# Block 2's S5 recurrence: scan instructions between two rotations, with a table of rotations made on GpSimd

## The chip, the core and the metric

The kernel runs on one core of one Trainium2 chip. Time is microseconds (us) of device time for one execution; less is better. The core has five engines, each with its own queue of instructions in a fixed order: TensorE (PE in the profile; its weight loads PEld), VectorE (DVE), ScalarE (ACT), GpSimd (POOL) and SyncE (SP), which issues most DMA transfers. An engine takes its next instruction when all earlier ones of its queue have begun and the semaphores that it waits for are up.

## What is computed

Two transformer blocks over 256 tokens and 2048 channels, in fp32. Block 1: differential attention and RWKV-7, gated branches, a gated FFN. Block 2: a mixer of S5, stick-breaking attention and NSA, cross attention, a convolutional FFN. The change touches S5, and by the order of instructions the gated branches of block 1. Cut to these:

```python
# block 1
mix = (gates[..., :D_MODEL] * (o_a @ w_branch_a[l])
       + gates[..., D_MODEL:] * (o_b @ w_branch_b[l])) @ w_out[l]
# block 2: S5, a diagonal complex state per group: 32 groups x 64 states, 256 steps
delta = jnp.exp(log_dt)[:, None]
mag = jnp.exp(lr * delta)
ar = mag * jnp.cos(li * delta)
ai = mag * jnp.sin(li * delta)
xr_in = jnp.einsum('btgc,gpc->btgp', ug, br)
xi_in = jnp.einsum('btgc,gpc->btgp', ug, bi)
_, _, sr, si = lax.associative_scan(_complex_affine, (a_r, a_i, xr_in, xi_in), axis=1)
y = jnp.einsum('btgp,gcp->btgc', sr, c_re) - jnp.einsum('btgp,gcp->btgc', si, c_im)
```

The states obey x(t) = a x(t-1) + b(t) with the same complex a at all steps. The 2048 complex states are 16 tiles of 128.

## The kernel before

**Products.** Every large fp32 product is three products in a format that TensorE runs faster: a weight tile W (128 x 1024 numbers, 512 KB) is read by SP, ScalarE copies it to WH (L163), VectorE makes the rest WL = W - WH (L164), and TensorE multiplies WH with both parts of the activations and WL with the high part (L146 to L148 in `gemm_steps`, L210, L211, L213 in `gemm_t`). So TensorE needs a split of VectorE for each W tile.

**Order.** The program is written as generators. Each `yield` of a gemm is a tick, and a tick advances six lanes of side work that were put there by `spawn`. From what is written so, a scheduler makes one static order for each engine, by its own estimate of when an instruction can run and by priorities (splits and evictions have a high one). An instruction can so come out ahead of the code that surrounds it in the program. `drain` ticks on until a lane is empty.

**Block 1, `mix1` (L973).** `w_br_b`'s outputs are gated and kept in `tb`. Then `w_br_a` runs in 8 blocks nb of 256 columns. Behind each block come two times: ScalarE copies a half of the result (L990), VectorE adds the other (L991), GpSimd multiplies with the gate tile `gr` (L992, tile `md`, four buffers), VectorE adds `tb` (L1025), ScalarE and VectorE make the high and the low part for the next gemm, `w_out` (L1026, L1027). The lane 3 runs `params()` meanwhile: block 2's S5 parameters (L1457 is their helper) and NSA's biases, kept in a DRAM tensor `pd`. The FFN, `ffn1` (L1132), follows.

**Block 2, S5 (`s5`, L1553).** `states()` makes the inputs b of the 16 tiles (TensorE, L1572), copied to SBUF by ScalarE (L1575). `scan(0)` runs the recurrence of nine tiles on VectorE, `scan(1)` that of seven on GpSimd, both with the helper `cma` (L1593), eight operations for one complex multiply-add: 15 steps inside 16 chunks of 16 tokens (128x144 and 128x112 elements), 15 steps from chunk to chunk (128x9 and 128x7), and a correction of all tokens (128x450 and 128x225), 280 operations on VectorE and 272 on GpSimd. `out()` multiplies with C. The lanes run this beside block 2's first gemm and beside stick-breaking attention (L1948 and following) and the compression of NSA's keys (L1891 to L1906; L1900 on VectorE makes the input of L1906).

Of the kernel before, what the change touches and what calls it, by code (L numbers as in the profile page):

```python
# [33 lines left out]
S5_V = 9  # L34
S5_Y = ((2, 1, 4), (2, 1, 6))
# [7 lines left out]
class K:  # L43
# [1088 lines left out]
    def ffn1(self, fp, xr, xa):  # L1132
        nc, tc = self.nc, self.tc
        acc = fp.tile([128, 2, D], F32, tag="acc", name="acc2")
        fin = self.post_norm(fp, acc, "g_ffn_post")
        parts = [range(0, 4), range(4, 8), range(8, 11)]
        first = True
        for pi, blocks in enumerate(parts):
# [43 lines left out]
            def ev_o(nb, P, hs=(0, 1)):  # L1182
                if pi == 2:
                    return fin(nb, P, hs, add=True)
                for h in range(2):
# [3 lines left out]
                    else:  # L1189
# [259 lines left out]
    def s5_params(self, sp):  # L1449
# [39 lines left out]
        PW = S([128, 2, 16, 16], "s5pw")  # L1489
        PR, PI = PW[:, 0], PW[:, 1]  # L1490
        ar, ai = PR[:, :, 0], PI[:, :, 0]
        tt(ar, mg, cs, mul)
        tt(ai, mg, sn, mul)
        tmp = [S([128, 16, 16], f"s5t{k}") for k in range(2)]

        def cmul(o, a, b, n):
            x, y = tmp[0][:, :, :n], tmp[1][:, :, :n]
            tt(x, a[0], b[0], mul)
            tt(y, a[1], b[1], mul)
            tt(o[0], x, y, sub)  # L1500
            tt(x, a[0], b[1], mul)
            tt(y, a[1], b[0], mul)
            tt(o[1], x, y, add)
        n = 1
        while n < 16:
            last = tuple(p[:, :, n - 1:n].to_broadcast([128, 16, n]) for p in (PR, PI))
            cmul((PR[:, :, n:2 * n], PI[:, :, n:2 * n]), (PR[:, :, 0:n], PI[:, :, 0:n]), last, n)
            n *= 2
            yield 3
# [30 lines left out]
        BT = S([128, 4, 2, 128], "s5bt")  # L1540
# [9 lines left out]
        for name, t in (("pw", PW), ("c2", C2), ("bt", BT)):  # L1550
            self.pd_out(name, t)

    def s5(self, sp):  # L1553
# [12 lines left out]
        def states():
            for t in [n for m in range(8) for n in (S5_V + m if S5_V + m < 16 else None, m) if n is not None] + list(range(8, S5_V)):
                p = int(t >= S5_V)
                q, kt = t % 4, t // 4
                ps = self.pst()  # L1570
                for k in range(2):
                    nc.tensor.matmul(ps[:, k * 256:k * 256 + 256], BT[32 * q:32 * q + 32, kt, k], uT[32 * q:32 * q + 32, kt],  # L1572
                                     start=True, stop=True, tile_position=(32 * q, 0))
                for k in range(2):
                    nc.scalar.activation(X[p][k][:, t - parts[p][1]], ps[:, k * 256:k * 256 + 256], AF.Copy)  # L1575
                yield

        def scan(p):
            E, n0, n1 = parts[p]
            n = n1 - n0  # L1580
            ts = slice(n0, n1)
            mul, add, sub = ALU.mult, ALU.add, ALU.subtract
            tmp = [S([128, 450], f"s5t{p}{k}") for k in range(2)]
            x5 = [x.rearrange("p t (c i) -> p t c i", c=16) for x in X[p]]

            def cma(dst, src, cf, shape):

                a = [tm[:, :math.prod(shape)] for tm in tmp]
                v = [q.rearrange("p (a b c) -> p a b c", a=shape[0], b=shape[1]) if len(shape) > 2 else
                     q.rearrange("p (a b) -> p a b", a=shape[0]) for q in a]  # L1590
                for o, a, b, op in ((v[0], src[0], cf[0], mul), (v[1], src[1], cf[1], mul), (dst[0], dst[0], v[0], add), (dst[0], dst[0], v[1], sub),
                                    (v[0], src[1], cf[0], mul), (v[1], src[0], cf[1], mul), (dst[1], dst[1], v[0], add), (dst[1], dst[1], v[1], add)):
                    E.tensor_tensor(o, a, b, op=op)  # L1593
            ab = [q[:, ts, 0:1].to_broadcast([128, n, 16]) for q in (PR, PI)]
            for i in range(1, 16):
                cma([x[:, :, :, i] for x in x5], [x[:, :, :, i - 1] for x in x5], ab, [n, 16])
                yield S5_Y[p][0]
            a16 = [q[:, ts, 15:16] for q in (PR, PI)]
            for c in range(1, 16):
                cma([x[:, :, c, 15:16] for x in x5], [x[:, :, c - 1, 15:16] for x in x5], a16, [n, 1])  # L1600
                yield S5_Y[p][1]
            for t0 in range(0, n, 2):
                m = min(2, n - t0)
                tl, tg = slice(t0, t0 + m), slice(n0 + t0, n0 + t0 + m)
                cma([x[:, tl, 1:16, 0:15] for x in x5],
                    [x[:, tl, 0:15, 15:16].to_broadcast([128, m, 15, 15]) for x in x5],
                    [q[:, tg, None, 0:15].to_broadcast([128, m, 15, 15]) for q in (PR, PI)], [m, 15, 15])
                yield S5_Y[p][2]
# [2 lines left out]
        def scans():
            self.spawn(3, scan(0))
            self.spawn(4, scan(1))
            yield
# [713 lines left out]
```

## Time and profile before

| | us |
|---|---|
| median of 3 runs (lowest, highest) | 3426.7 (3416.67, 3427.69) |
| the profiled execution | 3433.04 |
| its span in the trace | 3431.3 |
| TensorE busy | 3297.2 |
| VectorE busy | 2269.6 |
| GpSimd busy | 686.9 |

The span runs from the first to the last instruction of the trace; the execution's own time is 1.7 us longer. [...] In a timeline each row is one instruction, or several of one kind in a row (x2), with its start, its length, and in brackets how long the engine stood idle before it and what it waited for.

### The profile page before, as it was taken

To read this page: it belongs to the slowest core of one execution; us is meant where nothing else is said; L and a number is where in the kernel's file an instruction comes from. 1 tells how busy PE (TensorE), PEld (TensorE's weight loads), DVE (VectorE), ACT (ScalarE), POOL (GpSimd) and SP (SyncE) were. 2 spreads that over 40 slices of the span, in tenths; PEclk is the share of its full clock that TensorE was granted. 3 is DMA by queue.
4 is the path that set the end of the run, shared out by engine and by line. 5 is a ranking of instruction groups with operands and counts; after the bars stand their busy time and mean duration, and the time that the engine had idled before them with its cause. 6 is when DMAs were issued, how large, how long until landed. Compare 5 with 4: busy or idle time off the path is not lost.

```text
span 3431.3 us, 50392 instructions
## 1 busy us (share of the span) xinstructions
PE 3297.2 (96%) x18954; PEld 2743.5 (80%) x18954; DVE 2269.6 (66%) x3636; ACT 1710.4 (50%) x2675; POOL 686.9 (20%) x882
## 2 busy tenths in 40 slices
PE   8999999999999999999999999789999999999998
PEld 7887877877888888888888877567677888888886
DVE  5776787756667656545555565986777675666576
ACT  5545455444545445444444444256545554454453
POOL 0203123421111201100100113920121321111021
PEclk9999999999999999999999999989999999999999
DMA  6553544646556774566566564336356466666664
GB/s 215 155 176 102 160 133 130 194 155 215 185 176 226 236 257 135 184 191 190 186 190 192 187 223 144 99 106 207 125 184 207 135 185 191 188 187 192 190 186 154
DMA packets 177765, 607.04 MB, mean 177 GB/s; under 512 B 22427, under 2 KB 27372, under 8 KB 176752
## 3 DMA queue, kind: packets, MB, share of 16 engines
q1 hardware_dynamic: 168800, 580.25, 53.8%
q0 software_dynamic: 7856, 21.94, 2.0%
q8 instruction: 149, 2.44, 0.3%
q10 hardware_dynamic: 864, 1.62, 0.1%
q14 instruction: 96, 0.79, 0.1%
HBM read 584.29 MB, written 22.59 MB: 177 GB/s over the span
## 4 chain that ended last, share of the span: by engine, by line
PE 72%; DVE 8%; issue 8%; DMA 3%; ACT 2%; POOL 1%; DVEq 0%; POOLq 0%; ACTq 0%; SPq 0%
PE pm L211 25%; PE pm L210 12%; PE pm L146 9%; PE pm L147 9%; PE pm L148 9%; DVE WL L164 2%; PE ps L65 1%; DVE s5x L1593 1%; ACT WH L163 1%; PE pm L213 1%; DMA T<-dT 1%; DVE s5t L1593 1%; PE ps L1572 0%; DMA dT<-TM 0%; PE ps L1854 0%
## 5 line engine op out<-in xcount | busy, mean ns | idle before, releaser
L164 DVE TENSOR_TENSOR WL<-W,WH 128x1024 fp32r<-128x1024 f32 (+2 forms) x1016 | 1268.1, 1249 | 863.6 <-ACT WH L163 858.1
L211 PE MATMUL pm<-HL,WH 128*128 128x512 f32 x4928 | 1745.5, 401 | 8.8 <-ACT WH L163 4.0
L163 ACT ACTIVATE WH<-W 128x1024 fp32r<-128x1024 f32 (+2 forms) x1016 | 1066.9, 1051 | 1059.4 <-PE pm L148 444.7
L210 PE MATMUL pm<-HL,WL 128*128 128x256 f32 x4620 | 1313.6, 284 | 8.4 <-DVE WL L164 6.4
L211 PEld LDWEIGHTS pm<-HL,WH 128*128 128x128 f32 x4928 | 913.2, 189 | 212.6 <-DVE pt L496 7.7
L210 PEld LDWEIGHTS pm<-HL,WL 128*128 128x128 f32 x4620 | 875.3, 189 | 35.7 <-DVE WL L164 10.4
L147 PE MATMUL pm<-WL,HL 128*128 128x512 f32 (+1 forms) x1472 | 579.4, 394 | 17.5 <-DVE WL L164 17.5
L146 PE MATMUL pm<-WH,HL 128*128 128x512 f32 (+1 forms) x1472 | 585.4, 399 | 1.2 <-ACT WH L163 1.2
L148 PE MATMUL pm<-WH,HL 128*128 128x512 f32 (+1 forms) x1472 | 577.0, 392 | 0.7 <-DVE HL L1097 0.7
L147 PEld LDWEIGHTS pm<-WL,HL 128*128 128x128 f32 x1472 | 278.4, 189 | 79.1 <-DVE WL L164 23.3
L146 PEld LDWEIGHTS pm<-WH,HL 128*128 128x128 f32 x1472 | 277.7, 189 | 60.0 <-ACT WH L163 2.0
L148 PEld LDWEIGHTS pm<-WH,HL 128*128 128x128 f32 x1472 | 278.2, 189 | 58.3 <-DVE HL L1097 1.1
L2122 POOL TENSOR_TENSOR fcv<-fcv,fcv 128x256 f32<-128x256 f32 x44 | 51.8, 1176 | 547.4 <-DVE fcv L2109 547.4
L1155 POOL TENSOR_TENSOR sg<-sg,spr 128x256 f32<-128x256 f32 x44 | 45.9, 1060 | 391.2 <-ACT sg L1154 391.2
L213 PE MATMUL pm<-HL,WL 128*128 128x256 f32 x308 | 87.0, 282 | 0.8 <-DVE WL L164 0.8
L1164 POOL TENSOR_TENSOR HL<-fu,HL 128x256 fp32r<-128x256 f32 x44 | 48.3, 1118 | 195.2 <-ACT HL L1163 195.2
L1593 POOL TENSOR_TENSOR s5t<-s5x,PW 128x112 f32<-128x112 f32 (+3 forms) x136 | 71.8, 547 | 60.8 <-ACT s5x L1575 60.8
L2108 DVE SCALAR_TENSOR_TENSOR fcv<-fu,cw,fcv 128x255 f32<-128x255 f32 x88 | 53.1, 603 | 32.6 <-ACT fcv L2107 32.6
L2107 ACT ACTIVATE fcv<-fu,cw 128x256 f32<-128x256 f32 x88 | 52.4, 596 | 40.2 <-DVE fu L2106 40.2
L213 PEld LDWEIGHTS pm<-HL,WL 128*128 128x128 f32 x308 | 58.5, 190 | 13.5 <-DVE WL L164 1.5
L1593 POOL TENSOR_TENSOR s5x<-s5x,s5t 128x112 f32<-128x112 f32 (+3 forms) x136 | 68.7, 527 | 0.2
L1593 DVE TENSOR_TENSOR s5x<-s5x,s5t 128x144 f32<-128x144 f32 (+3 forms) x140 | 66.2, 473 | 1.5
(504 smaller groups left out, 3218.3 us busy)
## 6 DMA issues: line engine op xcount, KB each, us to landing
W<-in_w_ffi SPq DMA_DIRECT2D x176, 512.0 KB, 3.6
W<-in_w_up SPq DMA_DIRECT2D x176, 512.0 KB, 4.1
W<-in_w_rkv SPq DMA_DIRECT2D x96, 512.0 KB, 3.5
W<-in_w_qkv SPq DMA_DIRECT2D x96, 512.0 KB, 3.6
W<-in_w_ffo SPq DMA_DIRECT2D x88, 512.0 KB, 3.5
W<-in_w_down SPq DMA_DIRECT2D x88, 512.0 KB, 4.3
W<-in_w_gate SPq DMA_DIRECT2D x64, 512.0 KB, 4.1
W<-in_w_out SPq DMA_DIRECT2D x64, 512.0 KB, 4.3
```

The costliest lines, as they stand in the source:

```text
L146: nc.tensor.matmul(o, a, WH[:, j], start=(k == 0), stop=False)
L147: nc.tensor.matmul(o, a, WL[:, j], start=False, stop=False)
L148: nc.tensor.matmul(o, b, WH[:, j], start=False, stop=(k == kts - 1))
L163: self.nc.scalar.activation(WH, W, AF.Copy)
L164: self.gated(self.nc.vector.tensor_tensor(WL, W, WH.bitcast(F32), op=ALU.subtract))
L210: nc.tensor.matmul(o[:, 0, ts], WL[:, kk, c], x[:, 0, ts], start=False, stop=False)
L211: nc.tensor.matmul(o[:, :, ts], WH[:, kk, c], x[:, :, ts], start=(k == 0), stop=(k == 15))
L213: nc.tensor.matmul(o[:, 0, ts], WL[:, kk, c], x[:, 0, ts], start=False, stop=False)
L1593: E.tensor_tensor(o, a, b, op=op)
L2107: nc.scalar.activation(c, u, AF.Identity, scale=cw[:, 2, ct:ct + 1], bias=cw[:, 3, ct:ct + 1])
L2108: nc.vector.scalar_tensor_tensor(c[:, 1:], u[:, 0:255], cw[:, 1, ct:ct + 1], c[:, 1:], op0=ALU.mult, op1=ALU.add)
L2122: nc.gpsimd.tensor_tensor(c, c, gs[i], op=ALU.mult)
```

## The change

- The parameters: besides the magnitude `mg` of a, VectorE makes `un`, the unit rotation of a and its powers 2, 4, ..., 128, each brought back to length one. Both go to `pd`. The powers 1 to 16 of a, `pw`, go.
- `s5_table` (new, spawned on lane 3 at the start of `ffn1`): GpSimd makes the unit rotations of all 256 steps for the 16 tiles, in 8 groups of two tiles, by doubling: from n steps to 2n with four operations, two of 4n elements and two of 2n, for n = 1 to 128. Each group ends with a DMA of 512 KB into `pd` from GpSimd's queue. Each `yield 3` is three ticks.
- `s5`: for each tile, VectorE turns the inputs back by the table (two products of 128x512 with the result in PSUM, two of 128x256), runs two real scans along the 256 tokens (`tensor_tensor_scan`, with `mg` as factor), and GpSimd turns them forward again (two products of 128x512, two of 128x256). GpSimd also issues the 16 loads of 256 KB of the table. The copies by ScalarE and the recurrence by `cma` go. The work of a pair of tiles is spread over ticks by `S5_Y`, four ticks a tile.

```diff
-S5_V = 9
-S5_Y = ((2, 1, 4), (2, 1, 6))
+S5_Y = (1, 1, 2)
...
     def ffn1(self, fp, xr, xa):
         nc, tc = self.nc, self.tc
         acc = fp.tile([128, 2, D], F32, tag="acc", name="acc2")
+        self.spawn(3, self.s5_table())
...
+        self.drain(3)
         z = self.hl_both(self.hA)
...
+        self.pd_out("mg", mg)
+
+        un = S([128, 8, 2, 16], "s5un")
+        V.tensor_copy(un[:, 0], u)
+        for n in range(1, 8):
+            a, b, c, d = un[:, n - 1, 0], un[:, n - 1, 1], un[:, n, 0], un[:, n, 1]
+            tt(t0, a, a, mul)
+            tt(t1, b, b, mul)
+            tt(c, t0, t1, sub)
+            V.scalar_tensor_tensor(d, a, 2.0, b, op0=mul, op1=mul)
+            tt(t0, c, c, mul)
+            tt(t1, d, d, mul)
+            tt(t0, t0, t1, add)
+            V.tensor_scalar(t0, t0, -0.5, 1.5, op0=mul, op1=add)
+            tt(c, c, t0, mul)
+            tt(d, d, t0, mul)
+            yield 3
+        self.pd_out("un", un.rearrange("p n k t -> p (n k t)"))
...
+    def s5_table(self):
+
+        nc = self.nc
+        mul, add, sub = ALU.mult, ALU.add, ALU.subtract
+        ro = PD_OFF["rot"][0]
+        with self.tc.tile_pool(name="rt", bufs=1, reuse_waits="tile", side="right") as sp:
+            un = sp.tile([128, 8, 2, 16], F32, name="s5un")
+            self.pd_in(un.rearrange("p n k t -> p (n k t)"), "un")
+            yield 3
+            for g in range(8):
+                gs = slice(2 * g, 2 * g + 2)
+                R = sp.tile([128, 2, 2, 256], F32, tag="R", bufs=2, name=self.nm("s5rt"))
+                nc.gpsimd.memset(R[:, :, 0, 0:1], 1.0)
+                nc.gpsimd.memset(R[:, :, 1, 0:1], 0.0)
+                for k in range(8):
+                    n = 1 << k
+                    a, b = (sp.tile([128, 2, 2, 128], F32, tag=t, name=self.nm("s5ro"))[:, :, :, :n] for t in "ab")
+                    cb, sb = (un[:, k, x, gs, None, None].to_broadcast([128, 2, 2, n]) for x in range(2))
+                    R0, R1 = R[:, :, :, 0:n], R[:, :, :, n:2 * n]
+                    for o, x, y, op in ((a, R0, cb, mul), (b, R0, sb, mul), (R1[:, :, 0], a[:, :, 0], b[:, :, 1], sub),
+                                        (R1[:, :, 1], a[:, :, 1], b[:, :, 0], add)):
+                        nc.gpsimd.tensor_tensor(o, x, y, op=op)
+                    yield 3
+                nc.gpsimd.dma_start(self.pd[:, ro + 1024 * g:ro + 1024 * g + 1024], R.rearrange("p t k n -> p (t k n)"))
...
+        def rot(t):
+            R = sp.tile([128, 2, T], F32, tag="s5r", bufs=4, name=self.nm("s5r"))
+            nc.gpsimd.dma_start(R, self.pd[:, ro + 512 * t:ro + 512 * t + 512].rearrange("p (k t) -> p k t", k=2))
+            return R
...
+                    nc.vector.tensor_tensor(a, p3, cb, op=mul)
+                    nc.vector.tensor_tensor(b, p3, sb, op=mul)
+                    yield S5_Y[0]
+                    nc.vector.tensor_tensor(a[:, 0], a[:, 0], b[:, 1], op=add)
+                    nc.vector.tensor_tensor(a[:, 1], a[:, 1], b[:, 0], op=sub)
+                    yield S5_Y[1]
+                    for k in range(2):
+                        nc.vector.tensor_tensor_scan(a[:, k], mg[:, t:t + 1].to_broadcast([128, T]), a[:, k], 0.0, op0=mul, op1=add)
+                    nc.gpsimd.tensor_tensor(X[:, t], a, cb, op=mul)
+                    nc.gpsimd.tensor_tensor(b, a, sb, op=mul)
+                    nc.gpsimd.tensor_tensor(X[:, t, 0], X[:, t, 0], b[:, 1], op=sub)
+                    nc.gpsimd.tensor_tensor(X[:, t, 1], X[:, t, 1], b[:, 0], op=add)
+                    yield S5_Y[2]
```

The lines of `mix1` stand one lower in the changed kernel: L992 is L991 there, L1025 is L1024, L164 is L163.

**What moves.** GpSimd's queue in `w_br_a`, before, from the gate products (`md`) of block nb = 4 to those of nb = 7 and what follows them:

```order
L992 TENSOR_TENSOR md_11405<-md_11405,gr_11313 128x256
L992 TENSOR_TENSOR md_11412<-md_11412,gr_11313 128x256
L992 TENSOR_TENSOR md_11511<-md_11511,gr_11419 128x256
...
L992 TENSOR_TENSOR md_11723<-md_11723,gr_11631 128x256
L992 TENSOR_TENSOR md_11730<-md_11730,gr_11631 128x256
L1081 TENSOR_TENSOR xr<-xr,acc_11749 128x512 x2
```

The same queue now, from the end of the table's fourth group (`s5rt` is the table, `s5ro` its products) and nb = 4 to the first product of nb = 5:

```order
L1586 TENSOR_TENSOR s5ro_14137<-s5rt_13813,s5un 128x512
L991 TENSOR_TENSOR md_11460<-md_11460,gr_11368 128x256
L1586 TENSOR_TENSOR s5rt_13813<-s5ro_14136,s5ro_14137 128x2x128 x2
L1588 DMA pd<-s5rt_13813 128x1024
L991 TENSOR_TENSOR md_11467<-md_11467,gr_11368 128x256
L1586 TENSOR_TENSOR s5ro_14176<-s5rt_14173,s5un 128x4
...
L1586 TENSOR_TENSOR s5ro_14798<-s5rt_14535,s5un 128x512
L991 TENSOR_TENSOR md_11566<-md_11566,gr_11474 128x256
```

Between the second product of nb = 4 and the first of nb = 5 now stand the table's fifth and most of its sixth group. The first table operation comes behind the first product of nb = 2, the last DMA ahead of the two products of nb = 7; no table operation is left behind them, in the FFN.

VectorE's queue in the same stage, before, at block nb = 5 (L991 and L1025 lie before and behind GpSimd's product, WL is a split):

```order
L991 TENSOR_TENSOR md_11511<-pm_11421,md_11511 128x256
L1025 TENSOR_TENSOR md_11511<-md_11511,tb 128x256
L991 TENSOR_TENSOR md_11518<-pm_11422,md_11518 128x256
L164 TENSOR_TENSOR WL_11574<-W_11575,WH_11573 128x1024
L1027 TENSOR_TENSOR HL_10817<-md_11511,HL_10817 128x256
L1025 TENSOR_TENSOR md_11518<-md_11518,tb 128x256
L164 TENSOR_TENSOR WL_11596<-W_11597,WH_11595 128x1024
```

and now:

```order
L990 TENSOR_TENSOR md_11566<-pm_11476,md_11566 128x256
L990 TENSOR_TENSOR md_11573<-pm_11477,md_11573 128x256
L1024 TENSOR_TENSOR md_11566<-md_11566,tb 128x256
L1024 TENSOR_TENSOR md_11573<-md_11573,tb 128x256
L163 TENSOR_TENSOR WL_11629<-W_11630,WH_11628 128x1024
L1026 TENSOR_TENSOR HL_10842<-md_11566,HL_10842 128x256
L1026 TENSOR_TENSOR HL_10842<-md_11573,HL_10842 128x256
L163 TENSOR_TENSOR WL_11651<-W_11652,WH_11650 128x1024
```

The readers of GpSimd's products stand ahead of the next splits in both; at nb = 5 both readers now stand ahead of the block's third split.

VectorE's queue where block 2's S5 begins, before (`s5x` are the states, `s5t` products):

```order
L1593 TENSOR_TENSOR s5t_19460<-s5x_19089,PW 128x144
L1593 TENSOR_TENSOR s5t_19461<-s5x_19088,PW 128x144
L1593 TENSOR_TENSOR s5x_19089<-s5x_19089,s5t_19460 128x144
L1593 TENSOR_TENSOR s5x_19089<-s5x_19089,s5t_19461 128x144
L1593 TENSOR_TENSOR s5t_19460<-s5x_19088,PW 128x144
L164 TENSOR_TENSOR WL_19533<-W_19534,WH_19532 128x1024
```

and now, one pair of tiles (L1632 are the scans, `s5r` is the table's tile):

```order
L163 TENSOR_TENSOR WL_19755<-W_19756,WH_19754 128x1024
L1625 TENSOR_TENSOR s5a_19692<-ps_19682,s5r_19652 128x512
L1626 TENSOR_TENSOR s5b_19693<-ps_19682,s5r_19652 128x512
L1625 TENSOR_TENSOR s5a_19750<-ps_19683,s5r_19654 128x512
L1628 TENSOR_TENSOR s5a_19692<-s5a_19692,s5b_19693 128x256
L1629 TENSOR_TENSOR s5a_19692<-s5a_19692,s5b_19693 128x256
L1632 SCALAR_TENSOR_TENSOR s5a_19692<-s5mg,s5a_19692 128x256 x2
L163 TENSOR_TENSOR WL_19785<-W_19786,WH_19784 128x1024
```

The small operations of the recurrence are replaced by seven longer ones between two splits.

## Rows read from the trace of the kernel before

**Rows 1.** The page, part 1: busy time of each engine, share, instructions.
```profile
PE 3297.2 (96%) x18954; PEld 2743.5 (80%) x18954; DVE 2269.6 (66%) x3636; ACT 1710.4 (50%) x2675; POOL 686.9 (20%) x882
```
**Rows 2.** Windows around block 2's S5: stretch, length, busy times, PEclk, DMA.
```profile
2089.00:2125.00 36.00, 36.00 (x164) 25.41 (x163) 10.50 (x11) 17.08 (x38) 8.12 (x16) 1.00 0.30 92
2125.00:2223.60 98.60, 78.83 (x357) 58.93 (x355) 97.33 (x238) 31.33 (x41) 98.60 (x227) 0.95 0.35 111
2223.60:2244.60 21.00, 0.01 (x2) 0.04 (x1) 20.86 (x23) 0.38 (x1) 21.00 (x22) 0.57 0.00 0
2244.60:2256.00 11.40, 11.40 (x72) 10.79 (x73) 9.81 (x29) 5.85 (x8) 7.80 (x11) 0.50 0.31 94
sum 167.00, PE 126.24 PEld 95.17 DVE 138.50 ACT 54.64 POOL 135.52; mean PE 31.56 PEld 23.79 DVE 34.62 ACT 13.66 POOL 33.88
```
**Rows 3.** The same four windows, line L1593 alone, their sum.
```profile
sum 167.00, DVE 94.35 POOL 134.99; mean DVE 23.59 POOL 33.75
```
**Rows 4.** Waits in 2125 to 2262: engine, line, releaser, us, times, longest.
```profile
PE ps L1906 <- issue: 21.0, 1, 21.0
PE pm L147 <- DVE WL L164: 16.8, 11, 2.3
```
**Rows 5.** Windows of `mix1`: parameters, part of `w_br_a`, `w_out` and on.
```profile
1080.00:1120.00 40.00, 36.02 (x201) 30.54 (x200) 34.43 (x91) 20.39 (x27) 9.33 (x9) 1.00 0.81 274
...
1149.00:1209.00 60.00, 60.00 (x337) 52.08 (x337) 40.04 (x55) 30.23 (x44) 14.35 (x12) 1.00 0.66 198
1209.00:1290.00 81.00, 80.81 (x357) 66.62 (x356) 45.22 (x42) 38.87 (x48) 0.00 (x0) 1.00 0.76 253
```
**Rows 6.** Timeline of GpSimd in `w_br_a`, blocks nb = 2, 3 and 7.
```profile
1148.98 0.74 POOL L992 TENSOR_TENSOR md<-md,gr 128x256 f32<-128x256 f32 x1 [7.97 <-DVE md L991]
1150.60 1.66 POOL L992 TENSOR_TENSOR md<-md,gr 128x256 f32<-128x256 f32 x1 [0.87 <-DVE md L991]
1160.28 0.74 POOL L992 TENSOR_TENSOR md<-md,gr 128x256 f32<-128x256 f32 x1 [8.02 <-DVE md L991]
...
1205.45 0.74 POOL L992 TENSOR_TENSOR md<-md,gr 128x256 f32<-128x256 f32 x1 [8.03 <-DVE md L991]
```
**Rows 7.** Timeline of VectorE in `w_br_a`, block nb = 2.
```profile
1149.76 0.42 DVE L1025 TENSOR_TENSOR md<-md,tb 128x256 f32<-128x256 f32 x1 [0.86 <-POOL md L992]
...
1150.44 1.22 DVE L164 TENSOR_TENSOR WL<-W,WH 128x1024 fp32r<-128x1024 f32 x1
```
**Rows 8.** Timeline of SP's queue in `w_br_a`: four issues in a row.
```profile
1141.46 7.46 SPq L162 DMA_DIRECT2D W<-in_w_br_a  x4
```
**Rows 9.** Timeline of GpSimd in S5: two operations of each size.
```profile
2118.40 0.83 POOL L1593 TENSOR_TENSOR s5t<-s5x,PW 128x112 f32<-128x112 f32 x2
...
2216.51 0.38 POOL L1593 TENSOR_TENSOR s5t<-s5x,PW 128x7 f32<-128x7 f32 x2
2216.84 0.37 POOL L1593 TENSOR_TENSOR s5x<-s5x,s5t 128x7 f32<-128x7 f32 x2
...
2224.05 1.92 POOL L1593 TENSOR_TENSOR s5t<-s5x,PW 128x450 f32<-128x450 f32 x2
```
**Rows 10.** Timeline of VectorE in S5.
```profile
2129.08 1.44 DVE L164 TENSOR_TENSOR WL<-W,WH 128x1024 fp32r<-128x1024 f32 x1
...
2224.04 1.97 DVE L1593 TENSOR_TENSOR s5t<-s5x,PW 128x9 f32<-128x9 f32 x2
...
2249.10 0.17 DVE L1593 TENSOR_TENSOR s5t<-s5x,PW 128x9 f32<-128x9 f32 x1
```
**Rows 11.** Groups by line and form: busy us, mean ns of one.
```profile
L1062 DVE TENSOR_TENSOR acc<-pm,rowv 128x512 f32<-128x512 f32 x8 | 5.5, 690 | 3.8 <-ACT junk L1061 3.7
L226 DVE SCALAR_TENSOR_TENSOR bqk<-pm,bqk 128x256 f32<-128x256 f32 x8 | 3.4, 419 | 6.0 <-ACT bqk L225 6.0
L1755 DVE RECIPROCAL ngt<-ngt 128x96 f32<-128x96 f32 x1 | 0.8, 753 | 0.0
L1104 POOL DMA_DIRECT2D xsp<-xr x8 | 4.3, 548 | 0.0
```

More of the change, by code (lines that the diff above doesn't have):

```diff
@@ L1488, in s5_params @@
         yield 2
[L1489 to L1493, printed above, removed]
-        tmp = [S([128, 16, 16], f"s5t{k}") for k in range(2)]
[L1496 to L1509, printed above, removed]
+        ab = S([128, 2, 16], "s5a")
+        ar, ai = ab[:, 0], ab[:, 1]
+        u = S([128, 2, 16], "s5u")
+        tt(t0, cs, cs, mul)
+        tt(t1, sn, sn, mul)
+        tt(t0, t0, t1, add)
+        V.tensor_scalar(t0, t0, -0.5, 1.5, op0=mul, op1=add)
+        tt(u[:, 0], cs, t0, mul)
+        tt(u[:, 1], sn, t0, mul)
+        tt(ar, mg, u[:, 0], mul)
+        tt(ai, mg, u[:, 1], mul)
+        self.pd_out("mg", mg)
[9 more added lines that the diff above has]
+            tt(t1, d, d, mul)
+            tt(t0, t0, t1, add)
+            V.tensor_scalar(t0, t0, -0.5, 1.5, op0=mul, op1=add)
+            tt(c, c, t0, mul)
+            tt(d, d, t0, mul)
+            yield 3
+        self.pd_out("un", un.rearrange("p n k t -> p (n k t)"))
+        tmp = [S([128, 16, 16], f"s5t{k}") for k in range(2)]
         tt(t0, lr, lr, mul)
@@ L1539, in s5_params @@
         V.tensor_scalar(C2[:, 1], C2[:, 1], -1.0, None, op0=mul)
-        BT = S([128, 4, 2, 128], "s5bt")
+        BT = sp.tile([128, 4, 2, 128], F32, tag="s5bt", name="s5bt")
         yield 3
@@ L1555, in s5 @@
         S = lambda shape, name: sp.tile(shape, F32, name=name)
-        PW, BT = S([128, 2, 16, 16], "PW"), sp.tile([128, 4, 2, 128], F32, tag="s5c", name="BTs")
-        for name, t in (("pw", PW), ("bt", BT)):
+        BT, mg = sp.tile([128, 4, 2, 128], F32, tag="s5c", name="BTs"), S([128, 16], "s5mg")
+        for name, t in (("mg", mg), ("bt", BT)):
             self.pd_in(t, name)
-        PR, PI = PW[:, 0], PW[:, 1]
         uT = self.s5z = S([128, 4, T], "s5uT")
-        left = [0, 1]
-        parts = ((nc.vector, 0, S5_V), (nc.gpsimd, S5_V, 16))
@@ L1564, in s5 @@
-        X = [[sp.tile([128, n1 - n0, T], F32, name=self.nm("s5x")) for k in range(2)] for _, n0, n1 in parts]
+        left = [0]
+        X = S([128, 16, 2, T], "s5x")
+        mul, add, sub = ALU.mult, ALU.add, ALU.subtract
+        ro = PD_OFF["rot"][0]
+        def rot(t):
+            R = sp.tile([128, 2, T], F32, tag="s5r", bufs=4, name=self.nm("s5r"))
+            nc.gpsimd.dma_start(R, self.pd[:, ro + 512 * t:ro + 512 * t + 512].rearrange("p (k t) -> p k t", k=2))
+            return R
@@ L1566, in states @@
         def states():
[L1567 to L1570, printed above, removed]
+            Rs = [rot(0), rot(1)]
+            yield 2
+            for t0 in range(0, 16, 2):
+                pss = [self.pst() for _ in range(2)]
                 for k in range(2):
[L1572 to L1608, printed above, removed]
@@ new lines, in states @@
+                    for d in range(2):
+                        t = t0 + d
+                        q, kt = t % 4, t // 4
+                        nc.tensor.matmul(pss[d][:, k * 256:k * 256 + 256], BT[32 * q:32 * q + 32, kt, k], uT[32 * q:32 * q + 32, kt],
+                                         start=True, stop=True, tile_position=(32 * q, 0))
+                nxt = [rot(t0 + 2), rot(t0 + 3)] if t0 < 14 else []
+                for d in range(2):
+                    t, R = t0 + d, Rs[d]
+                    cb, sb = (R[:, k:k + 1].to_broadcast([128, 2, T]) for k in range(2))
+                    p3 = pss[d].rearrange("p (k t) -> p k t", k=2)
+                    a, b = (sp.tile([128, 2, T], F32, tag=tg, bufs=2, name=self.nm(tg)) for tg in ("s5a", "s5b"))
+                    nc.vector.tensor_tensor(a, p3, cb, op=mul)
[11 more added lines that the diff above has]
+                    yield S5_Y[2]
@@ L1609, in scan @@
+                Rs = nxt
             left.pop()
[L1611 to L1614, printed above, removed]
         ut = self.np_.tile([128, 2, 512], F32, tag="nqt", bufs=2, name="s5ut")
@@ L1617, in s5 @@
             nc.scalar.activation(ut[:, h], self.u5[h], AF.Copy)
-        self.spawn(0, self.tok_T(ut, uT))
-        self.spawn(0, states())
-        self.spawn(0, scans())
+        self.spawn(3, self.tok_T(ut, uT))
+        self.spawn(3, states())
         def out():
@@ L2149 @@
 PD_OFF, PD_N = {}, 0
-for _k, _n in (("pw", 512), ("c2", 1024), ("bt", 1024), ("bc", 480)):
+for _k, _n in (("mg", 16), ("un", 256), ("rot", 8192), ("c2", 1024), ("bt", 1024), ("bc", 480)):
     PD_OFF[_k] = (PD_N, _n)
```

9 lines of the change are left out of this document (4 added, 5 removed).

## The prediction

> **What bounds the kernel now.** I read the page first. TensorE is busy for 96% of the span of 3431.3 us [rows 1], so there is no slack in which lost TensorE time could be regained; a change counts by what it gives to or takes from TensorE. Next the stretches around block 2's S5 [rows 2]. Until 2125 TensorE has no gap, then it is busy 78.83 of 98.6 us, nothing of 21 us, and runs 11.4 us at clock 0.50 of full, the lower of its two levels, right after that idle time. VectorE is busy 97.33 of 98.6, 20.86 of 21 and 9.81 of 11.4 there: it is the bound of this stage. The same stretches with the recurrence's line L1593 alone [rows 3] say what fills it: 94.35 of VectorE's 138.50 us. The waits [rows 4] show how that reaches TensorE: PE waits 16.8 us in all for splits WL, and once for 21.0 us at L1906, whose input (L1900) stands behind the recurrence in VectorE's queue.
>
> Then the stage in which, by the new order of instructions, GpSimd's queue changes most: block 1's `w_br_a` gemm. Before, TensorE loses nothing there (60.00 of 60 us), VectorE is busy 40.04 and GpSimd 14.35 [rows 5]. GpSimd does a pair of gate products L992 per block of 256 columns, 11.3 us from pair to pair [rows 6].
>
> **Gain: block 2's S5.** First the most that can come back. What TensorE did in these 167 us, at full speed, is 36.0 + 78.83 x 0.95 + 11.4 x 0.50 = 117 us, so 50 us at the most.
>
> VectorE's new work: 138.50 - 94.35 = 44 us stay. Each of 16 tiles of states gets two products of 128x512 from PSUM (0.69 each by the nearest row, L1062), two of 128x256 (0.42, L226), and two scans over 256 [rows 11]. No scan instruction stands in this trace. From below, an operation of that shape takes 0.42; from above, the slowest kind on this engine, the reciprocal, 0.753 for 96 elements and so 2.0 for 256 [rows 11]. I take 0.45, near the row of the same shape, since the scan is a multiply and an add like L226. That makes 1.38 + 0.84 + 0.90 = 3.1 us a tile, 50 us for 16, and 94 in all. GpSimd's share, two products of 512 and two of 256 a tile, comes by the prices below to 3.4 us, 55 us in all, plus 16 DMA issues at 0.55 [rows 11]; it runs beside VectorE and stretches it (a WL takes 1.44 beside it [rows 10], 1.22 alone [rows 7]): I add 18 us of holding up. VectorE then needs some 112 us where TensorE needs 117. Two engines so evenly loaded don't pack without gaps: rows of VectorE's new order have three splits and both rotations of a tile in turn, so I leave 14 us of loss. **Gain 36 us, from 25 (scan 0.75) to 48.** The 32 copies on ScalarE that go, and 16 loads of 256 KB in the stage, lie beside other work: DMA is at 0.30 to 0.35 there [rows 2].
>
> [...]
>
> **Loss: the table in `w_br_a`.** The table is written in the FFN's code, but the order of instructions puts all eight groups on GpSimd's queue ahead of, and between, the gate products of blocks nb 2 to 7; the FFN holds none of it. The products' readers, L1024 on VectorE, stand ahead of later splits WL (so TensorE's own operands) on that engine's queue; before, one such reader waits 0.86 for its product [rows 7]. GpSimd late means VectorE blocked, then TensorE without WL.
>
> When it starts: the read of `un` stands on SP's queue behind the W tile that before was the third of four issued from 1141.46 to 1148.92 [rows 8], so near 1146; its data I take to be there 3 us later (a guess of no weight, since GpSimd comes to the table behind the product at 1148.98). Start 1149 to 1150.
>
> What a group costs: 32 operations, two of 4n and two of 2n elements for n = 1, 2, ..., 128: 3060 elements. GpSimd starts two operations of 7 elements in 0.33, 0.165 each, and one of 450 takes 0.96 (1.92 for two) [rows 9]: 0.152 fixed and 1.8 ns an element. So 4.9 + 5.5 = 10.4, and 0.55 for a DMA issue and 0.3 for two memsets (bounded by two small operations): 11.3 us. Eight groups 90. Eleven products of 0.74 [rows 6] lie between: 8.
>
> What VectorE adds: the two engines hold each other up. A product takes 0.74 where VectorE runs something short and 1.65 beside a WL [rows 6, 7]; a 128x9 operation on VectorE takes 0.17 alone and near 1.0 each beside GpSimd's 450-element ones [rows 9, 10]. About 18 WL fall into the stretch, 0.91 each, and some 22 smaller operations at about 0.3: 23 us. GpSimd is through with the first seven and a half groups near 1263; then come product nb 6, the last two steps of TensorE and the pair nb 7: about 1271, where the last pair began at 1205.45 [rows 6]. **Loss 65 us.** As a rule for other prices: eight groups, 8 of products and the holding up, less 56 that these blocks took anyhow. From below: without holding up, 42. From above: by the rows of 112 elements (0.83 for two [rows 9], 2.4 ns an element) a group is 1.8 dearer, 14 in all: 80. Low clock at the restart (11.4 us of it cost 5.7 in rows 2) stays within these ends; between the blocks it hides in the waiting. Nothing later gives it back: TensorE is busy 80.81 of the 81 us that follow [rows 5].
>
> [...] The 450-element row shows 1.8 here, a broadcast input among its operands. [...]
>
> **The rest.** The parameters get some 50 more operations of 128x16 on VectorE, in a stretch where it is busy 34.43 of 40 and TensorE 36.02 [rows 5]; at 0.17 (the row of 128x9 alone [rows 10]) that is 8.5 us, most of it into VectorE's gaps: +2 on TensorE, 0 to 5.
>
> **Sum.** 65 + 2 - 36 = +31 us on the profiled run of 3433.04, some 3464; that run lies 6.3 above the median of 3426.7, on which +31 makes **3458 us**.
>
> **Rivals.**
> *A, the engines don't hold each other up* in `w_br_a`, because VectorE stands still most of that time, waiting for GpSimd: the loss is 42, and with the same in S5 the gain is 48: 42 + 2 - 48 = -4, 3423. Not slower. For it: a blocked VectorE can't hold anything up. Against it: the splits have to be made anyhow, and the row 1.65 is just such a split. It decides from where the loss falls to the gain: by the rule above at a group price of 7.4 us with the holding up (gain 36), of 11.8 without (gain 48).
> *B, the scan is as slow as the reciprocal's rate*, 2 us: VectorE gets 32 x 1.55 = 50 us more, the stage is its own again with 160 us, the gain 5 to 10: 3485. Nothing in the profile excludes it.
> *C, the table is hidden*, as its place in the FFN's code would have it: loss 0, +2 - 36, so 3393. It would need another order than the one that stands; the one way left is that VectorE's products wait less than I think because TensorE has blocks in hand. But four buffers `md` and the order allow two blocks at most.
> *D, GpSimd dearer* (112-element or two-input price) with a small gain of 25: 80 + 3 - 25 = +58, 3485.
>
> **How the numbers follow.** My case has 0.58; A 0.15; B 0.09; C 0.05; D 0.13. Predicted 3458. The range 3418 to 3486 takes in A and B and D at their near ends and leaves out C and the far ends. Within 0.3% of the median, 10 us, a measurement of this kernel can't tell a change from none. Faster by more: all of C, a third of A and a little of my case, 0.12. Within it: half of A and the low end of mine, 0.14. Slower: 0.74.
>
> **What would show it.** In the changed kernel's profile: pairs of gate products on GpSimd near 1177, 1202, 1229, 1254 and 1270 and not every 11.3 us; VectorE's wait at L1024 for GpSimd the longest of that stretch; TensorE busy about half of 1150 to 1270. No table operation after 1300. In S5 (some 67 us later) a TensorE busy for over 85%, no idle 21 us ahead of L1906's successor, and a scan row under 0.75. The gain is wrong if a scan row is over 1 us or VectorE still has no idle time there; the loss is wrong if GpSimd's operations of 512 take far from 1.1, or if TensorE works on while L1024 waits.

## The result, and the profile after

| | before | changed |
|---|---|---|
| median, us (lowest, highest) | 3423.19 (3416.67, 3427.69) | 3466.22 (3458.33, 3469.72) |
| ratio | 1 | 1.0124, 95% interval 1.0098 to 1.0150 |
| profiled execution, us | 3433.04 | 3464.75 |

The change makes the kernel slower, by 1.24% or 42 us. The forecast was 3458, slower by 31. The two profiled executions lie only 32 us apart, because that of before is 10 us above its median; so I compare stages within the profiles and take totals from the ratios.

How far the changed kernel runs behind, at the same instruction in both traces (start in the changed kernel less start before):

| place | lag, us |
|---|---|
| first parameters of S5, L1476 (1088.5 before) | +1.9 |
| first gate product of `w_br_a` (1124.5) | +5.7 |
| last gate product of `w_br_a` (1207.1) | +79.8 |
| last gate product of block 1's FFN, L1155 (1970.7) | +79.1 |
| first product of NSA's compression, L1906 (2244.6) | +39.5 |
| NSA's scores, L1811 (2364.4) | +36.9 |
| end of the span (3431.3) | +31.6 |

So 74 us are lost inside `w_br_a`, the FFN keeps the lag, and S5 with what runs beside it gives 42 back by NSA's scores. The last 5 us fall in stages that the change doesn't touch; drifts of up to 5 us stand there between before and other traces below too (4.6 in e4), so I give them to no part of the change.

The stage of the loss. The timeline of GpSimd in the changed kernel, gate products only (start, length; between them stand table operations), which answers to [rows 6]:

```profile
1154.00 0.75 POOL L991 TENSOR_TENSOR md<-md,gr 128x256 f32<-128x256 f32 x1
1158.95 0.75 POOL L991 TENSOR_TENSOR md<-md,gr 128x256 f32<-128x256 f32 x1
...
1187.62 1.42 POOL L991 TENSOR_TENSOR md<-md,gr 128x256 f32<-128x256 f32 x2
...
1215.82 0.72 POOL L991 TENSOR_TENSOR md<-md,gr 128x256 f32<-128x256 f32 x1
...
1245.60 0.72 POOL L991 TENSOR_TENSOR md<-md,gr 128x256 f32<-128x256 f32 x1
...
1273.50 0.72 POOL L991 TENSOR_TENSOR md<-md,gr 128x256 f32<-128x256 f32 x1
...
1285.25 0.73 POOL L991 TENSOR_TENSOR md<-md,gr 128x256 f32<-128x256 f32 x1 [2.08 <-DVE md L990]
1286.86 0.73 POOL L991 TENSOR_TENSOR md<-md,gr 128x256 f32<-128x256 f32 x1 [0.88 <-DVE md L990]
```

These are blocks nb = 2 to 7: nb = 3 comes 34 us after nb = 2, then a pair every 28 to 30 us, where it was every 11.3. The last pair comes 11.75 after the one ahead and alone waits for VectorE again (2.08): the table is through by then. The pairs before it wait for nothing but their place on the queue, so TensorE's lower clock in this stretch (0.74, below) is hidden behind GpSimd. The waits of the changed kernel from 1120 to 1285 (us in all, times, longest) name the chain from GpSimd to TensorE:

```profile
DVE md L1024 <- POOL md L991: 84.8, 10, 21.9
...
PE pm L209 <- DVE WL L163: 67.2, 6, 17.9
...
POOL s5ro L1586 <- DMA s5un<-pd: 2.1, 1, 2.1
```

And VectorE's timeline at nb = 5, in the order that the prediction speaks of: a reader of GpSimd's product, 18 us idle, and the split behind it:

```profile
1227.74 0.42 DVE L990 TENSOR_TENSOR md<-pm,md 128x256 f32<-128x256 f32 x1 [0.55 <-ACT md L989]
1246.36 1.24 DVE L1024 TENSOR_TENSOR md<-md,tb 128x256 f32<-128x256 f32 x1 [18.19 <-POOL md L991]
1248.22 0.93 DVE L1024 TENSOR_TENSOR md<-md,tb 128x256 f32<-128x256 f32 x1 [0.62 <-POOL md L991]
1249.07 1.74 DVE L163 TENSOR_TENSOR WL<-W,WH 128x1024 fp32r<-128x1024 f32 x1
```

The windows answer to [rows 5] and, the second, to [rows 2]: `w_br_a` with the table, and S5 (126 us for what took 167). A row has the stretch and its length, the busy time and the number of instructions of PE, PEld, DVE, ACT and POOL, then PEclk, the mean clock granted to TensorE as a share of its full clock, the DMA share and GB/s:

```profile
1153.85:1281.00 127.15, 62.10 (x301) 52.88 (x300) 36.26 (x46) 25.41 (x38) 114.11 (x289) 0.74 0.32 110
```
```profile
2168.00:2294.00 126.00, 112.51 (x586) 89.12 (x585) 120.12 (x151) 44.39 (x59) 95.46 (x77) 0.93 0.47 148
```

In the first, TensorE works half of the time, at a mean clock of 0.74; VectorE is busy 36 of 127 us, so it stands still and isn't overloaded. In the second TensorE is busy 112.5 of 126, and VectorE 120: still the fuller engine, and for the first 102 us without a gap:

```profile
2168.00:2270.00 102.00, 91.17 (x430) 71.25 (x428) 101.17 (x123) 34.99 (x43) 79.03 (x62) 0.95 0.48 150
```

### The profile page after: what moved, and what is told of

Its sections match the earlier page's. It is cut to its first block, busy times and chain, and to the rows that moved or that the text cites. A ratio compares the mean times of both kernels' runs of the same rounds, so it can differ in the third digit from the quotient of the medians.

```text
span 3462.9 us, 50363 instructions
## 1 busy us (share of the span) xinstructions
PE 3287.1 (95%) x18954; PEld 2739.1 (79%) x18954; DVE 2247.5 (65%) x3505; ACT 1696.6 (49%) x2641; POOL 754.1 (22%) x970
## 4 chain that ended last, share of the span: by engine, by line
PE 69%; DVE 8%; issue 8%; POOL 5%; DMA 4%; ACT 2%; DVEq 0%; POOLq 0%; SPq 0%; ACTq 0%
PE pm L210 23%; PE pm L209 11%; PE pm L145 9%; PE pm L146 9%; PE pm L147 9%; DVE WL L163 2%; POOL s5ro L1586 2%; POOL s5rt L1586 1%; PE ps L64 1%; ACT WH L162 1%; DMA T<-dT 1%; PE pm L212 1%; PE ps L1877 1%; DMA W<-in_w_out 0%; DMA dT<-TM 0%
## 5 line engine op out<-in xcount | busy, mean ns | idle before, releaser
L163 DVE TENSOR_TENSOR WL<-W,WH 128x1024 fp32r<-128x1024 f32 (+2 forms) x1016 | 1274.5, 1256 | 836.9 <-ACT WH L162 831.5
L1155 POOL TENSOR_TENSOR sg<-sg,spr 128x256 f32<-128x256 f32 x44 | 45.9, 1061 | 389.6 <-ACT sg L1154 389.6
L1024 DVE TENSOR_TENSOR md<-md,tb 128x256 f32<-128x256 f32 x16 | 10.3, 646 | 85.6 <-POOL md L991 85.6
L1145 ACT ACTIVATE fu<-pm 128x256 f32<-128x256 f32 x88 | 33.9, 386 | 64.2 <-PE pm L210 64.2
L1586 POOL TENSOR_TENSOR s5ro<-s5rt,s5un 128x8 f32<-128x8 f32 (+7 forms) x128 | 55.7, 455 | 6.5 <-DMA s5un<-pd 2.1
```

What stands on the lines that cost most here:

```text
L163: self.gated(self.nc.vector.tensor_tensor(WL, W, WH.bitcast(F32), op=ALU.subtract))
L1586: nc.gpsimd.tensor_tensor(o, x, y, op=op)
```

## The experiments

Two theories of the loss were to be told apart. **Queue**: VectorE, and behind it TensorE, waits for gate products that stand behind table operations in GpSimd's queue. **Holding up**: the engines slow each other down wherever the table runs beside VectorE.

| run | ratio to before | 95% interval |
|---|---|---|
| changed kernel | 1.0124 | 1.0098 to 1.0150 |
| e1, table kept in the FFN | 0.9921 | 0.9899 to 0.9943 |
| e2, table alone, old S5 | 1.0206 | 1.0187 to 1.0225 |
| e3, gate products on VectorE | 0.9928 | 0.9909 to 0.9947 |
| e4, table's arithmetic left out | 0.9888 | 0.9869 to 0.9908 |
| e5, table behind both FFN operations | 0.9889 | 0.9871 to 0.9908 |
| e6, e5 with eight ticks a tile | 0.9906 | 0.9884 to 0.9928 |
| e7, e5 with products for scans | 0.9865 | 0.9844 to 0.9887 |
| e8, half of the table | 1.0006 | 0.9992 to 1.0021 |
| e9, e5 with five ticks a tile | 0.9881 | 0.9861 to 0.9901 |
| e10, e5 with six ticks a tile | 0.9881 | 0.9860 to 0.9902 |
| e11, e5 with one of four forward products | 0.9850 | 0.9832 to 0.9868 |

**e1, the table held in the FFN.** Each table operation gets an order-only dependence on the FFN's latest gate product, an instruction of the same engine. In the trace the table's 256 operations have one semaphore wait in all, as in the changed kernel.

```diff
-                        nc.gpsimd.tensor_tensor(g, g, R, op=ALU.mult)
+                        self.lg = nc.gpsimd.tensor_tensor(g, g, R, op=ALU.mult)
...
-                        nc.gpsimd.tensor_tensor(o, x, y, op=op)
+                        self.after(nc.gpsimd.tensor_tensor(o, x, y, op=op), self.lg)
```

> Only the place of the table on GpSimd's queue differs from the changed kernel: each operation of it is ordered behind the FFN's latest gate product L1155, so it can't come out ahead of w_br_a's products. Queue theory (the loss is VectorE, and behind it TensorE, waiting for gate products that stand behind table operations): last pair of gate products again near 1210, the 74 us lost in w_br_a come back, 3394 us, ratio near 0.991. Rival (GpSimd and VectorE hold each other up wherever the table runs): the FFN pays 20 to 40 us instead, some 3420.

Measured 0.9921 (3400.85 us): the same work, placed elsewhere on one queue, is 69 us faster than the changed kernel and 27 faster than before. It lands at the queue theory's end, 7 us short. A wait of TensorE in the FFN says where the 7 are:

```profile
PE pm L147 <- POOL HL L1165: 6.5, 1, 6.5
```

TensorE waits once, at the first product of `w_ffo`, for a low part that GpSimd makes and that stands behind table operations: the same trap, smaller.

**e2, the table without the new S5.** The kernel before, plus parameters, `s5_table` and its spawn; the old S5 doesn't read the table.

> The kernel before with the new parameters and the table spawned as in the changed kernel, S5 itself as before (the table is not used). Queue theory: the order puts six and a half groups ahead of the last pair of gate products (seven and a half in the changed kernel), so some 64 us of loss and 3 of parameters: 3490 us, ratio 1.019. If part of the changed kernel's loss lay in its new S5, this would be nearer to 1.01.

Measured 1.0206, 71 us against 67 expected. The loss is there without a line of the new S5.

**e3, the gate products moved off GpSimd.**

```diff
-                    nc.gpsimd.tensor_tensor(d, d, g[:, i], op=ALU.mult)
+                    E.tensor_tensor(d, d, g[:, i], op=ALU.mult)
...
-                            total(P, i, d, g)
+                            total(P, i, d, g, nc.vector)
```

> The changed kernel with the gate products of w_br_a (16 of 128x256) on VectorE in place of GpSimd; the table runs in the same stretch on GpSimd, ahead of the FFN. Queue theory: nothing of VectorE waits for GpSimd there, the loss falls from 74 to 5 to 15 us (VectorE has 8.3 us of work per block of 11.3 and is held up by the table's operations), 3400 to 3410, ratio 0.994. Rival (the holding up is what costs): the loss stays above 45, over 3440.

Measured 0.9928. This run separates the theories best: the table runs in the same stretch, beside the same splits, with more work on VectorE, and TensorE loses next to nothing there. Its windows over the table's first 127 us, and then the wait in which the price reappears:

```profile
1153.00:1209.00 56.00, 56.00 (x318) 48.75 (x317) 43.53 (x59) 27.56 (x40) 49.65 (x93) 1.00 0.70 217
1209.00:1280.00 71.00, 70.22 (x307) 57.17 (x306) 47.48 (x41) 35.36 (x44) 66.59 (x115) 1.00 0.84 284
```
```profile
PE ps L64 <- POOL xr L1080: 13.0, 1, 13.0
```

TensorE is busy 56.00 of 56 with GpSimd busy 49.65, and 70.22 of the next 71 with GpSimd busy 66.59: holding up by itself costs TensorE next to nothing here, where VectorE has room (43.53 and 47.48). What is lost comes later and once: the next instruction of GpSimd that anybody waits for is the residual's sum L1080, now behind the end of the table at 1312.

**e4, no table arithmetic.** One memset and eight DMAs of a constant tile in place of 256 operations.

> The table's arithmetic is left out of the changed kernel: one memset and eight DMAs of a constant tile write it, so S5's rotations are by ones. Queue theory: as e1 within 10 us, 3390 to 3400, ratio 0.991; what e1 is above it is the price of the table hidden in the FFN. If the parameters or the 4 MB of transfers were the loss, it would stay near 3460.

Measured 0.9888. The new S5 with its parameters and its transfers is worth 38 us. Neither the parameters nor the 4 MB written and read are the loss.

**e5, held behind both operations of the FFN.**

```diff
-                        nc.gpsimd.tensor_tensor(fL[:, kk], u, fH[:, kk].bitcast(F32), op=ALU.subtract)
+                        self.lg = nc.gpsimd.tensor_tensor(fL[:, kk], u, fH[:, kk].bitcast(F32), op=ALU.subtract)
```

> As e1, with the table also ordered behind the FFN's latest low part L1164 (the other operation of GpSimd there). In e1 TensorE waits once for 6.5 us at the start of w_ffo for a low part that stands behind table operations. Queue theory: that wait goes and with it some 7 us, 3393, ratio near 0.990. If the FFN's price for the table (e1 against e4, 12 us) is the holding up of VectorE, it stays at 3400.

Measured 0.9889 (3391.60 us): the table is now free within what the runs can tell (e4 without it: 0.9888). The window over the FFN with the table in it:

```profile
1330.00:1640.00 310.00, 310.00 (x1652) 265.82 (x1651) 178.20 (x193) 149.72 (x203) 187.01 (x321) 1.00 0.67 204
```

GpSimd is busy 187 of 310 us beside VectorE's 178, and TensorE has no gap. This kernel leaves nothing out and is faster than both, by 1.1% and 2.3%.

**e8, half of the table** in the changed kernel's place: of groups 4 to 7 a memset in place of the 32 operations; the DMAs stay.

```diff
+                if g < 4:
...
+                else:
+                    nc.gpsimd.memset(R, 1.0)
+                    yield 24
```

> The changed kernel with the arithmetic of the last four of eight groups left out (a memset of a constant tile in its place, the DMAs stay); the table runs ahead of w_br_a's products as before. Queue theory: all groups are now through ahead of the pair of nb = 5, which comes near 1226 where it was due near 1188; nb 6 and 7 follow at TensorE's pace: loss some 40 in place of 74, 3432, ratio 1.002. A loss from holding up alone would halve to 37 too, so this tests the size per group (13 us with the pairs of dependent operations, against 11.3 of the prediction, which would make the loss 30).

Measured 1.0006: 40 us above e5, as expected from 13 us a group. GpSimd's timeline shows it, the first product of nb = 4 to 7: nb = 4 is still late by the table, the others follow, the last two at the old pace of 11.3.

```profile
1217.12 0.72 POOL L991 TENSOR_TENSOR md<-md,gr 128x256 f32<-128x256 f32 x1
...
1231.09 0.73 POOL L991 TENSOR_TENSOR md<-md,gr 128x256 f32<-128x256 f32 x1
...
1242.60 0.74 POOL L991 TENSOR_TENSOR md<-md,gr 128x256 f32<-128x256 f32 x1 [9.16 <-DVE md L990]
...
1253.89 0.74 POOL L991 TENSOR_TENSOR md<-md,gr 128x256 f32<-128x256 f32 x1 [8.03 <-DVE md L990]
```

I had expected nb = 5 near 1226; the pair came at 1231. What the run doesn't do is tell the queue from the holding up, as its expectation says; e3 did that.

**e7, what a scan costs.**

```diff
-                        nc.vector.tensor_tensor_scan(a[:, k], mg[:, t:t + 1].to_broadcast([128, T]), a[:, k], 0.0, op0=mul, op1=add)
+                        nc.vector.tensor_tensor(a[:, k], mg[:, t:t + 1].to_broadcast([128, T]), a[:, k], op=mul)
```

> e5 with each scan replaced by one plain product of 128x256 on VectorE: the recurrence is left out. The scans stand at 0.60 us from start to start, such a product at 0.34: 8 us less of VectorE. If VectorE bounds the S5 stage, 5 to 8 us faster than e5; if the scan's price lies beside TensorE's work, the same.

Measured 0.9865 against e5's 0.9889 (medians 3383.44 and 3391.60): 8 us, as 32 scans at 0.25 more than a product make. So time taken from VectorE here comes off the whole, one for one: VectorE still bounds the S5 stage. The two instructions (shortest/median/longest, ns), first of the changed kernel, then of e7:

```profile
L1632 DVE TENSOR_TENSOR_SCAN s5a<-s5mg,s5a x32: 657/678/1230, 2170.0 to 2287.1; 128x256 f32<-128x256 f32 x32
```
```profile
L1635 DVE TENSOR_TENSOR s5a<-s5mg,s5a x32: 409/412/959, 2096.7 to 2206.0; 128x256 f32<-128x256 f32 x32
```

**e11, what GpSimd's rotation costs VectorE.** Three of GpSimd's four operations per tile are left out; VectorE's instructions stay.

```diff
-                    nc.gpsimd.tensor_tensor(b, a, sb, op=mul)
-                    nc.gpsimd.tensor_tensor(X[:, t, 0], X[:, t, 0], b[:, 1], op=sub)
-                    nc.gpsimd.tensor_tensor(X[:, t, 1], X[:, t, 1], b[:, 0], op=add)
```

> e5 with three of GpSimd's four operations per tile of S5 left out (the forward rotation is not completed). VectorE's own instructions stay the same. If GpSimd holds VectorE up there (128x256 sums of 1.00 and 0.71 us where 0.42 is usual, splits of 1.53 where 1.23 is usual, some 25 us in all), the S5 stage loses VectorE's overload and 6 to 10 us come back against e5: 3383. If VectorE's own work is the limit, no change.

Measured 0.9850, 13 us under e5 where 6 to 10 were expected. VectorE's products from PSUM and one of its two sums per tile (groups by line and form: busy us, mean ns), e5, then e11's sum, the S5 stage of both by windows, and TensorE's waits in it (us in all, times, longest), e5's two largest and e11's only one:

```profile
L1632 DVE TENSOR_TENSOR s5a<-s5a,s5b 128x256 f32<-128x256 f32 x16 | 16.0, 998 | 0.0
...
L1628 DVE TENSOR_TENSOR s5a<-ps,s5r 128x512 f32<-128x512 f32 x16 | 10.9, 684 | 0.7 <-POOL s5b L1637 0.6
```
```profile
L1632 DVE TENSOR_TENSOR s5a<-s5a,s5b 128x256 f32<-128x256 f32 x16 | 6.6, 416 | 0.0
```
```profile
2095.00:2221.00 126.00, 113.23 (x583) 89.02 (x581) 120.06 (x150) 45.51 (x60) 95.45 (x77) 0.92 0.48 147
```
```profile
2095.00:2221.00 126.00, 124.44 (x677) 101.17 (x676) 109.39 (x165) 55.84 (x72) 36.96 (x29) 0.96 0.55 175
```
```profile
PE pm L146 <- DVE WL L163: 5.1, 4, 3.3
PE ps L1993 <- DVE ba L1988: 4.4, 1, 4.4
```
```profile
PE ps L1929 <- issue: 1.6, 1, 1.6
```

The same sum takes 998 ns on average beside all four of GpSimd's operations and 416 beside one, TensorE no longer waits for VectorE, and it goes from 113 to 124 of 126 us busy. So in S5, where VectorE is full, holding up has a price; in e3's `w_br_a`, where VectorE had room, it cost TensorE nothing. In the changed kernel's `w_br_a` it counts another way: it makes the table itself longer, and with it the queue (below).

**e6, e9, e10, other paces.** Only `S5_Y` differs from e5: (2, 2, 4), (1, 1, 3) and (1, 2, 3).

> e5 with the tiles of S5 at eight ticks each in place of four (S5_Y 2, 2, 4). In the changed kernel VectorE is busy 99.7% for 100 us of S5 and TensorE loses some 9 us there. If that is VectorE being just overfull, the same work over twice the time gives 5 to 9 us back against e5; if the loss is in fixed waits, or S5's end is late for what follows, nothing or worse.

> e5 with five ticks for a tile of S5 in place of four (S5_Y 1, 1, 3). At eight ticks (e6) S5's stage came out some 20 us ahead of e5 but the next stage gave all of it and more back, since its end waited for S5. If VectorE at four ticks is just overfull (99 of 102 us), five give 3 to 6 us against e5 with S5 still in time: 3387. If S5's end is already what the next stage waits for, no change or slower.

> e5 with six ticks for a tile (S5_Y 1, 2, 3). As e9: 3 to 8 us against e5 if S5 still ends in time; between e5 and e6 (3392 to 3397) if not.

Measured 0.9906, 0.9881 and 0.9881, against e5's 0.9889. At eight ticks S5 itself goes well, but the stretch from 2300 then does worse; two windows of e6, the S5 stretch and the stretch from 2300:

```profile
2100.00:2221.00 121.00, 118.74 (x660) 95.50 (x659) 101.42 (x126) 56.77 (x74) 61.31 (x50) 1.00 0.59 184
...
2300.00:2420.00 120.00, 102.46 (x643) 66.49 (x643) 83.27 (x190) 63.43 (x198) 30.58 (x35) 0.83 0.25 82
```

TensorE is busy 118.74 of 121 us, and then 102.46 of 120 (115.53 in e5's trace of that stretch). That the second is S5's late end, and which of its outputs is waited for, I haven't tested. Whether five or six ticks gain over four can't be told from these intervals.

## Why the prediction was right, and where its terms were off

**The step that decided held**: the table is not in the FFN, it stands on GpSimd's queue among the products of `w_br_a`, and VectorE's readers stand ahead of the splits. e1, e3 and e5 undo exactly that, in three ways, and the loss goes or moves to the next reader. Rival C (hidden) needed another order and would have been right with e5's order: 0.9889, where C said 3393.

**Start.** Forecast 1149 to 1150; the first table operation came at 1156.85. Five of the seven us are the lag that had built up (1154.00 for the product at 1148.98 before), 2.10 a wait for `un`, which I had put down as without weight.

**A group.** Forecast 11.3, measured 13.0: the row of the DMA issue that ends the second group, and that which ends the first, are 12.96 apart. What my sum lacked are waits between operations. In [rows 9] a pair of 7 elements starts 0.33 after the pair ahead, before that has ended (0.38). In the table a pair of 4 elements takes 0.35, and the next starts 0.08 behind its end, 0.43 after its start; the DMA issue waits 0.30 for the last pair. Sixteen pairs at 0.1 and that wait make 1.9; the two memsets, for which I had 0.3, fall into such a gap (1182.09) and cost nothing. Operations of [rows 9] also read what a pair ahead of them wrote, so that alone is not the difference; which it is, no run tests.

```profile
1174.03 0.60 POOL L1588 DMA_DIRECT2D pd<-s5rt  x1 [0.30 <-POOL s5rt L1586]
1174.65 0.35 POOL L1586 TENSOR_TENSOR s5ro<-s5rt,s5un 128x4 f32<-128x4 f32 x2
1175.08 0.35 POOL L1586 TENSOR_TENSOR s5rt<-s5ro,s5ro 128x2 f32<-128x2 f32 x2
...
1180.96 1.19 POOL L1586 TENSOR_TENSOR s5ro<-s5rt,s5un 128x256 f32<-128x256 f32 x2
...
1182.23 0.87 POOL L1586 TENSOR_TENSOR s5rt<-s5ro,s5ro 128x128 f32<-128x128 f32 x2
1183.18 2.04 POOL L1586 TENSOR_TENSOR s5ro<-s5rt,s5un 128x512 f32<-128x512 f32 x2
1185.29 1.40 POOL L1586 TENSOR_TENSOR s5rt<-s5ro,s5ro 128x256 f32<-128x256 f32 x2
1186.99 0.60 POOL L1588 DMA_DIRECT2D pd<-s5rt  x1 [0.30 <-POOL s5rt L1586]
```

The 1.8 ns an element held only as a mean of two prices. The products by `s5un`, which is broadcast, go from 1.19 to 2.04 for two when 256 elements become 512: 1.7 ns an element. The sums, with two full inputs, go from 0.87 to 1.40 when 128 become 256: 2.1 ns. With 2040 and 1020 of the 3060 elements the mean is 1.8.

**Holding up.** Forecast 23, measured 16: from 1156.85 to the last DMA's end at 1283.17 are 126.3 us, less eight groups (103.7) and nine products of 0.72 (6.5). The 18 splits that I had counted did meet the table, at about the price that I had; a split, and two operations of 2 elements beside it, which take 0.35 at 1175.08 above:

```profile
1220.30 1.21 DVE L163 TENSOR_TENSOR WL<-W,WH 128x1024 fp32r<-128x1024 f32 x1
```
```profile
1220.52 1.39 POOL L1586 TENSOR_TENSOR s5rt<-s5ro,s5ro 128x2 f32<-128x2 f32 x2
```

What was too dear are the smaller operations of VectorE, 22 at 0.3 in the sum. With each GpSimd instruction set against the shortest of its kind, nearly 16 us of delay lie beside splits and 1 us beside 26 smaller operations. **Rival A** (no holding up, since VectorE stands still) is out in this stage: VectorE stood still most of the time, but made its splits all the same. In S5 e11 shows the holding up too.

**The loss** came to 74 us where I had 65: 14 more for groups, 2 for the wait for `un` and 2 from the table's end to the last pair, less 7 of holding up and 2 for two products fewer. It lies within the bounds given (42 to 80). The pairs came later than the signs said for the same reasons: 1188, 1216, 1246, 1274 and 1285 where I had 1177, 1202, 1229, 1254 and 1270. **Rival D** had a group at 13.1, by a dearer element; the size is the measured one, the cause isn't, and its gain of 25 is not what came. Its 80 used the 112-element price, 2.4 ns; its two-input price had no row beside it, and the sums with two full inputs came to 2.1.

**The parameters**: +2 forecast, +3.8 in the profile, in 0 to 5. Lags of such a size come between two executions ahead of any change (e1 runs 6 us behind at the same place), so this term isn't settled.

**The gain** was 36 by my sum, 42 by the trace, so here two terms were wrong and offset each other. VectorE's was low: a scan stands at 0.60 from start to start and takes 0.66 alone, not 0.45, and up to 1.23 beside GpSimd; the six instructions of a tile come to 72.7 us of length for all tiles, not 50 and a part of 18; VectorE is busy 120 us in the stage, not 112. The 18 had a misread row under it: the split of 1.22 that I called alone [rows 7] is the one beside which the product took 1.66, so there GpSimd bore the delay.

TensorE's side was high, and this is the step that failed: 117 us of work and, as a guess, 14 of loss because two full engines don't pack, 131 in all. The stage took 126, 6 more than VectorE's 120. How much of that is TensorE's work can't be read this way: the same sum of busy time and clock gives 112.51 x 0.93 = 105 us for it in the changed kernel. Nor is 50 the most that can come back: e11 gained 13 us on e5, some 55 in all. One sign that I set against the gain came true, VectorE without idle time (101.17 of 102 us), and the gain was there all the same, so it was no sign.

A scan alone takes 0.66 against 0.41 for a product of the same shape, and e7 measures the price of the 32 scans over products at 8 us. The 0.75 for a scan at the low end of the gain stood in no row of before; the 32 scans of the changed kernel took 0.77 on average. **Rival B** (2 us a scan) is out.

By the profiles the total is within 1 us of the forecast, and that is luck: 9 more of loss and 2 more of parameters stand against 6 more of gain and the 5 of drift in stages that the change doesn't touch. By the ratios the forecast is 11 us short.

## What to carry to other kernels

Where a scheduler makes the order, work "written beside" a stage is not placed there: read its queue, and tie it by an order-only dependence to an instruction of that stage on the same engine, the last one that anybody waits for. An engine that is busy 20% (GpSimd before; 22% in the changed kernel) still sets the pace of what stands in its queue behind a long job; what counts is who waits for the next instruction there. Price a chain of small operations by rows in which each waits for the one ahead as it will in the new code, and ask of two engines that slow each other down whether the one that TensorE needs has room.

## What the runs showed of the hardware

In the table's chain on GpSimd a pair of small operations starts 0.08 us behind the end of the pair ahead, 0.43 after its start, where the recurrence of before has 0.33; a DMA issue on its queue waits 0.30 for the operation whose result it sends. In the table's operations an element costs GpSimd 2.1 ns in the sums, with two full inputs, and 1.7 in the products, with one input broadcast. A scan over 256 fp32 numbers on VectorE takes 0.66 us where a product takes 0.41 (the shortest of 32 each, changed kernel and e7). A sum of 128x256 with both inputs in SBUF takes 998 ns on average on VectorE beside four of GpSimd's operations a tile and 416 beside one (e5, e11), while products that read PSUM took 0.68 in both: of these instructions, the holding up falls on the first kind.
